# A causal mask as a bound on the score in the pass out of PSUM, and sixteen weight sums moved to layer 0's feed-forward

## The chip, the cores and the metric

The kernel runs on one core of one Trainium2 chip. The metric is the device time of one execution in microseconds (us), as the median of several runs; less is better.

The engines are named as in the profile: PE is TensorE (matrix multiply), PEld its weight loads, DVE is VectorE, ACT is ScalarE, POOL is GpSimd and SP is SyncE, which issues most transfers. POOL issues the rest. Each engine works through its own instructions in the order in which the program lists them.

## What is computed

One inference step of a two-layer decoder for a group of 1024 prompt tokens and 8 sample tokens, width 1024, all in float32. Layer 0 mixes by a gated linear recurrence beside attention into 256 memory tokens, layer 1 by stick-breaking attention over shared keys and values beside the same kind of memory attention. Each layer ends with a SwiGLU feed-forward of width 2816. The parts of the reference that the change touches:

```python
def swiglu(h, w_gu, w_down):
    gate, up = jnp.split(h @ w_gu, 2, axis=-1)
    return (jax.nn.silu(gate) * up) @ w_down
...
def stick_breaking(q, k, v, bias, q_pos, k_pos):
    ...
        z = jnp.einsum('bqhd,bkhd->bhqk', qi.astype(jnp.float32), kf) * scale + bf
        mask = (k_pos[None, :] < pi[:, None])[None, None]
        log_keep = jnp.where(mask, jax.nn.log_sigmoid(-z), 0.0)
        tail = lax.cumsum(log_keep, axis=3, reverse=True) - log_keep
        w = jnp.where(mask, jnp.exp(jax.nn.log_sigmoid(z) + tail), 0.0)
        return jnp.einsum('bhqk,bkhd->bqhd', w, vf)
```

## The kernel before

The prompt is worked in two groups of 512 tokens; group 1 also carries the 8 sample tokens, so its tiles are 520 wide. Every float32 matrix product is made of three products of rounded parts: a weight tile is loaded by SP (line 199), rounded by ACT (204), its remainder taken by DVE (205), and TensorE multiplies (218). Raw and split weights have five buffers each.

The program is written as generators, one for each piece of work. `weave` runs several of them together, each with a number that says into how many steps it is thought to fall; it always takes the one that is least far on. That sets the order of the instructions on each engine. A feed-forward is cut into parts (`PARTS`: 5, 5, 4, 4 and 4 tiles of 128 hidden columns).

Stick-breaking attention of a prompt group is `sb_prompt`. For each of four heads it goes through units of one or two query chunks of 128 tokens. The scores come into one of three PSUM banks (1314). DVE passes them out, adds the head's offset and bounds them at 44 (1319). ACT makes softplus of them, exp and then ln(1 + x) (1297, 1298). In the block of 128 x 128 on the diagonal DVE multiplies this by a 0/1 matrix `sm01` (1301), which takes away the tokens that may not be seen. A running sum from the right (1326), a subtraction (1328) and an exponential (1329) give the weights, and the diagonal block is multiplied by `sm01` once more. Then TensorE transposes (1338), ACT passes out of PSUM (1340) and TensorE multiplies by the values (1343). There are 32 diagonal blocks: four heads, two groups, four query chunks.

Memory attention of a prompt group (`mem_attn`) has scores at 854, their maximum at 859, a division at 871, transposes at 878. For the sample tokens, `sb_sample` and `mem_attn_sample` run on DVE: a key tile of 512 KB is loaded for each token (`c`; 941 for memory by SP, 953 by gathers on POOL for the paged keys and values, two halves each), the token's query is loaded spread over all partitions (`b<-qd`, 911), and DVE multiplies and reduces (912, 913). For the values it scales and adds (924, 925) and TensorE sums over the partitions (926). The tiles `c` have four buffers.

The second group's feed-forward is done with fewer products, from sums of blocks of the weights (`ffn_w`). Those sums are made by transfers from DRAM to DRAM that POOL issues: for each part eight steps, four of them copies or first terms (556) and four accumulating (554), in `weight_sums`. Ahead of each step stands a marker, a copy of one column of a tile that was just made (551, `mk`); POOL waits for that tile, and so the transfer starts no earlier. Layer 0 has sums for parts 2 to 4, layer 1 for all five parts. Layer 1's forty sums are used from the last stage on, in `ffn_w(1, ...)`.

The stages in which layer 1's sums stand before: sixteen (parts 0 and 1, 1.25 MB each) beside group 0's stick-breaking attention, eight (part 2, 1 MB) beside the weighted feed-forward of group 1 in layer 0, and sixteen (parts 3 and 4, 1 MB) beside group 1's stick-breaking attention and the samples' attention:

```python
    weave((chain(b0.sb(), b0.mem()), 25), (chain(f1.part(0), f1.part(1)), 18), (islice(ws, 16), 17))
...
    weave((chain(fw.part(2), fw.part(3), fw.part(4)), 24), (islice(ws, 8), 8))
```

The functions that the change touches:

Of the kernel before, what the change touches and what calls it, by code (L numbers as in the profile page):

```python
# [9 lines left out]
F32 = mybir.dt.float32  # L10
# [4 lines left out]
ALU = mybir.AluOpType  # L15
# [3 lines left out]
P = 128  # L19
# [4 lines left out]
def tile_decoder(  # L24
# [6 lines left out]
    nc = tc.nc  # L31
# [25 lines left out]
    const = pool("const", 1)  # L57
# [83 lines left out]
    ones = const.tile([P, P], F32, name="ones")  # L141
# [25 lines left out]
    def drain(*gens):  # L167
        for g_ in gens:
            for _ in g_:
                pass  # L170

    def chain(*gens):
        for g_ in gens:
            yield from g_

    def weave(*streams):

        live = [[0, n, g_] for g_, n in streams]
        while live:
            cur = min(live, key=lambda e: e[0] / e[1])  # L180
            cur[0] += 1
            try:
                next(cur[2])
            except StopIteration:
                live.remove(cur)
# [1111 lines left out]
        nc.scalar.activation(e[:, :w], zb[:, :w], AF.Exp)  # L1297
        nc.scalar.activation(e[:, :w], e[:, :w], AF.Ln, bias=1.0)

    def keep_strict(t):  # L1300
        nc.vector.tensor_mul(t, t, sm01)

    def sb_prompt(g, Qs, xo):

        units = [[(0, g), (2, g)], [(1, g)], [(3, g)]]
# [3 lines left out]
        def weights(h, kh, unit, first):  # L1309
            ps, spans, o = S(), [], 0  # L1310
            for c, s in unit:
                w = (c + 1) * P if s == g else G
                spans.append((c, s, o, w))
                nc.tensor.matmul(  # L1314
                    ps[:, o : o + w], Qs[h // 2][:, h % 2, c * P : (c + 1) * P], kh[:, s, :w], start=True, stop=True
                )
                o += w
            zb = B()
            nc.vector.tensor_scalar(zb[:, :o], ps[:, :o], biasp[:, h : h + 1], 44.0, op0=ALU.add, op1=ALU.min)
            e = B()  # L1320
            softplus(zb, e, o)
            for c, s, a, w in spans:
                if s == g:
                    keep_strict(e[:, a + w - P : a + w])
                d = e[:, a : a + w][:, ::-1]
                nc.vector.tensor_tensor_scan(d, d, d, first.get(c, 0.0), op0=ALU.add, op1=ALU.max)
                first[c] = e[:, a : a + 1]
            nc.vector.tensor_sub(zb[:, :o], zb[:, :o], e[:, :o])
            nc.scalar.activation(zb[:, :o], zb[:, :o], AF.Exp)
            for c, s, a, w in spans:  # L1330
                if s == g:
                    keep_strict(zb[:, a + w - P : a + w])
            return zb, spans, o

        def values(vh, po, zb, spans, n):
# [97 lines left out]
    with tc.issue_after(made[0].ins):  # L1433
        trif = const.tile([P, P], F32, name="trif")
        nc.gpsimd.affine_select(
            trif, ones, pattern=[[-1, P]], compare_op=ALU.is_ge, fill=0.0, base=0, channel_multiplier=1
        )

        sm01 = const.tile([P, P], F32, name="sm01")
        nc.gpsimd.affine_select(  # L1440
            sm01, ones, pattern=[[-1, P]], compare_op=ALU.is_gt, fill=0.0, base=0, channel_multiplier=1
        )
        sel = const.tile([P, NB, NB], F32, name="sel")
        nc.gpsimd.affine_select(
# [1 line left out]
            compare_op=ALU.is_equal, fill=0.0, base=0, channel_multiplier=0,  # L1446
# [61 lines left out]
    weave((a1.core(), 22), (f0.part(0), 9), (islice(w0, 8), 9))  # L1508
    a1.open()
    weave((a1.sample(), 6), (a1.gate(), 4), (f0.part(1), 9), (w0, 5))  # L1510
    weave((chain(a1.merge(), a1.mem()), 12), (a1.mem_sample(), 20), (chain(f0.part(2), f0.part(3)), 16))
    drain(f0.part(4))
    xk0, xb0 = [], []
    o1 = out_proj(1, 0, M)
    drain(o1.mm(a1.xo, 0, 1))
# [5 lines left out]
    weave((b0.heads(), 8), (o1.finish(), 17))  # L1521
    b0.open()
    f1 = ffn(1, 0, o1.x)
    ws = weight_sums(1, range(5))
    weave((chain(b0.sb(), b0.mem()), 25), (chain(f1.part(0), f1.part(1)), 18), (islice(ws, 16), 17))
    set_banks(True)
    fw = ffn_w(0, o1.x, (5, 6, 5), 2, False, f1.R)
# [13 lines left out]
    f0 = ffn(0, 1, o0.x)  # L1541
    weave(
        (chain(b1.sb(), b1.mem()), 45), (chain(b1.sb_sample(), b1.mem_sample()), 39),
        (chain(f0.part(0), f0.part(1), f0.part(2), f0.part(3)), 34), (ws, 17),
    )
    o1 = out_proj(1, 1, A, True)
    drain(o1.mm(b1.xo))
# [37 lines left out]
```

## Time and profile before

| | |
|---|---|
| median of three runs | 2513.66 us (2510.47 to 2513.87) |
| profiled execution | 2513.78 us; its span, first to last instruction, 2511.9 us |
| mean granted TensorE clock | 0.995 |
| busy | PE 98%, PEld 86%, DVE 64%, ACT 48%, POOL 5% of the span |
| DMA | 41.4% of sixteen engines' span for SP's queue, 13.4% for POOL's |

Where a line of the profile reads `x64 | 17.0, 287 | 15.1 <-ACT b L1298 11.5`, there were 64 such instructions, busy for 17.0 us together, 287 ns each in the mean; their engine had stood idle for 15.1 us just before them, and what ended 11.5 us of that was ACT's instruction of line 1298. In a line of waits, `PE s L1338 <- DVE b L1301: 5.0, 3, 4.5` says that PE's instruction of line 1338, which writes a tile `s`, waited 5.0 us in all for DVE's of line 1301, three times, at most 4.5 us. In a line by time, the first two numbers are the start and the duration in us, and the bracket is idle time and what ended it. The granted clock is the share of its full clock that TensorE was given.

### The profile page before, as it was taken

How to read it: one execution, taken by the hardware profiler on the slowest of the kernel's cores; microseconds unless marked ns; L12 is line 12 of the kernel's file. 1: busy time of each engine (PE TensorE's matmuls, PEld its weight loads, DVE VectorE, ACT ScalarE, POOL GpSimd, SP SyncE). 2: the span in 40 equal slices, each digit the busy share in tenths (PEclk: the TensorE clock that was granted, in tenths of full speed). 3: DMA queues.
4: the chain of work that ended last, by engine and by line, in shares of the span. 5: the costliest groups of instructions: out<-in, count | busy, mean ns of one | idle time of the engine just before them, and what ended most of it. 6: DMA issues, size and time to landing. Idle time of an engine off the chain costs nothing.

```text
span 2511.9 us, 40889 instructions
## 1 busy us (share of the span) xinstructions
PE 2467.7 (98%) x15455; PEld 2160.5 (86%) x15455; DVE 1609.2 (64%) x2900; ACT 1197.4 (48%) x2289; POOL 119.6 (5%) x187
## 2 busy tenths in 40 slices
PE   8999999999999999999999999999999999999998
PEld 6888888877877898999999989876677798999998
DVE  5766556654766576665655676776687538845666
ACT  5437543243433454554434554554454335554445
POOL 1000000000000000010100100021000000000000
PEclk9999999999999999999999999999999999999999
DMA  5355656554743447476767746575456643464552
GB/s 189 116 158 126 162 174 164 130 145 144 195 122 101 130 138 219 148 181 163 187 177 194 221 139 191 167 193 143 135 167 169 167 123 118 134 186 140 150 151 73
DMA packets 521550, 391.24 MB, mean 156 GB/s; under 512 B 19973, under 2 KB 459858, under 8 KB 521354
## 3 DMA queue, kind: packets, MB, share of 16 engines
q1 hardware_dynamic: 493194, 308.94, 41.4%
q0 software_dynamic: 28160, 79.70, 13.4%
q8 instruction: 121, 1.98, 0.3%
q14 instruction: 75, 0.61, 0.1%
HBM read 358.76 MB, written 101.11 MB: 183 GB/s over the span
## 4 chain that ended last, share of the span: by engine, by line
PE 90%; DVE 4%; DMA 3%; ACT 1%; issue 1%; SPq 0%; POOL 0%; DVEq 0%; ACTq 0%
PE mm L218 53%; PE q L499 11%; PE q L631 7%; PE q L453 2%; PE s L1150 2%; PE mm L1018 2%; DMA b<-qd 1%; PE s L1343 1%; PE s L885 1%; PE s L854 1%; PE mm L803 1%; PE mm L830 1%; PE s L1314 1%; PE q L663 1%; PE ns L926 1%
## 5 line engine op out<-in xcount | busy, mean ns | idle before, releaser
L218 PE MATMUL mm<-x,ws 128*128 128x512 f32 (+1 forms) x6624 | 1216.0, 340 | 2.4 <-DVE t L235 1.5
L218 PEld LDWEIGHTS mm<-x,ws 128*128 128x128 f32 x6624 | 1013.6, 189 | 155.5 <-issue 17.4
L204 ACT CAST ws<-w 128x512 fp32r<-128x512 f32 (+1 forms) x672 | 395.1, 589 | 616.8 <-PE mm L218 468.3
L205 DVE TENSOR_TENSOR ws<-w,ws 128x512 fp32r<-128x512 f32 (+1 forms) x672 | 435.1, 651 | 259.7 <-ACT ws L204 247.5
L218 PE MATMUL mm<-m,ws 128*128 128x512 f32 (+1 forms) x1536 | 329.3, 367 | 0.0
L218 PEld LDWEIGHTS mm<-m,ws 128*128 128x128 f32 x1536 | 255.1, 189 | 51.3 <-issue 1.9
L631 PE MATMUL q<-m,ws 128*128 128x260 f32 x1440 | 175.7, 283 | 0.0
L631 PEld LDWEIGHTS q<-m,ws 128*128 128x128 f32 x1440 | 173.4, 188 | 0.9 <-DVE t L522 0.5
L490 DVE TENSOR_TENSOR ws<-w,ws 128x512 fp32r<-128x512 f32 x164 | 112.4, 691 | 79.7 <-ACT ws L489 77.1
L489 ACT CAST ws<-w 128x512 fp32r<-128x512 f32 x164 | 101.4, 621 | 98.8 <-PE q L631 33.1
L499 PE MATMUL q<-x,ws 128*128 128x260 f32 x1008 | 134.3, 282 | 0.0
L499 PEld LDWEIGHTS q<-x,ws 128*128 128x128 f32 x1008 | 126.4, 188 | 0.0
L499 PE MATMUL q<-y,ws 128*128 128x260 f32 x912 | 119.3, 283 | 0.1
L499 PEld LDWEIGHTS q<-y,ws 128*128 128x128 f32 x912 | 113.5, 189 | 0.3 <-ACT q L506 0.3
L235 DVE TENSOR_SCALAR t<-mm 128x512 f32<-128x512 f32 (+1 forms) x70 | 48.4, 691 | 57.6 <-PE mm L218 57.3
L695 DVE TENSOR_TENSOR t<-t,mm 128x512 f32<-128x512 f32 (+1 forms) x54 | 37.2, 689 | 60.0 <-PE mm L218 59.9
L390 DVE TENSOR_TENSOR r<-r,mm 128x512 f32<-128x512 f32 (+1 forms) x72 | 49.4, 686 | 39.9 <-PE mm L218 39.0
L239 DVE TENSOR_TENSOR t<-t,t 128x512 f32<-128x512 f32 (+1 forms) x54 | 37.4, 693 | 55.4 <-ACT t L238 55.4
L226 DVE TENSOR_TENSOR m<-t,m 128x512 fp32r<-128x512 f32 (+1 forms) x88 | 61.0, 693 | 6.8 <-ACT m L225 5.3
L225 ACT CAST m<-t 128x512 fp32r<-128x512 f32 (+1 forms) x88 | 54.9, 624 | 21.7 <-DVE t L695 13.0
L453 PE MATMUL q<-x,ws 128*128 128x260 f32 x480 | 61.0, 288 | 3.7 <-DVE r L390 2.2
L258 DVE TENSOR_TENSOR st<-st,n 128x512 f32<-128x512 f32 (+1 forms) x91 | 62.4, 694 | 2.9 <-ACT n L257 1.5
(342 smaller groups left out, 2869.1 us busy)
## 6 DMA issues: line engine op xcount, KB each, us to landing
w<-in_w_gu SPq DMA_DIRECT2D x310, 256.0 KB, 3.2
w<-in_w_down SPq DMA_DIRECT2D x160, 256.0 KB, 2.9
wsum<-in_w_gu POOLq DMA_DIRECT2D x36, 1024.0 KB, 9.6
w<-wsum SPq DMA_DIRECT2D x94, 256.0 KB, 3.3
w<-in_w_in_a SPq DMA_DIRECT2D x80, 256.0 KB, 3.2
w<-in_w_o SPq DMA_DIRECT2D x64, 256.0 KB, 2.8
wsum<-in_w_gu POOLq DMA_DIRECT2D x12, 1280.0 KB, 10.5
wsum<-wsum POOLq DMA_DIRECT2D x12, 1024.0 KB, 6.6
```

Source lines behind the costliest of these rows:

```text
L204: nc.scalar.copy(ws[:, 0, :n, :], raw[:, :n, :])
L205: nc.vector.tensor_sub(ws[:, 1, :n, :], raw[:, :n, :], ws[:, 0, :n, :].bitcast(F32))
L218: nc.tensor.matmul(ps[:, a, : PW[g]], wt, xt[k][:, xi, o : o + PW[g]], start=(k == 0 and wi == 0), stop=(k == nk - 1 and wi == 2),)
L225: nc.scalar.copy(dst[0], src)
L226: nc.vector.tensor_sub(dst[1], src, dst[0].bitcast(F32))
L258: nc.vector.tensor_add(acc[:, :n], acc[:, :n], t[:, :n])
L453: ins = nc.tensor.matmul(pp[a][:, :h], wt, xt[k][:, xi, a * h : (a + 1) * h], start=(k == 0 and wi == 0), stop=(k == ND - 1 and wi == 2),)
L489: nc.scalar.copy(w[:, 0, :], src)
L490: nc.vector.tensor_sub(w[:, 1, :], src, w[:, 0, :].bitcast(F32))
L499: nc.tensor.matmul(ps[:, :h], w[:, wj, k * P : (k + 1) * P], x[:, xi, :], start=(first and k == 0 and wi == 0), stop=(k == 3 and wi == 2), ...
L631: nc.tensor.matmul(pp[a][:, :h], wt, mids[k][:, xi, a * h : (a + 1) * h], start=(k == 0 and wi == 0), stop=(k == nf - 1 and wi == 2),)
L1018: nc.tensor.matmul(pb[i][:, a, :], xt[k][:, xi, c * P : (c + 1) * P], ws[:, s, :], start=(k == 0 and wi == 0), stop=(k == ND - 1 and wi == 2),
```

## The change

The mask. A matrix `cap` of 128 x 128 holds 44 where a token may be seen and -300 where not; POOL fills it at the start. In the pass out of PSUM the diagonal block is taken by an instruction with three operands, which adds the offset and bounds the score by `cap` element by element. The columns beside it are passed as before, in an instruction of their own. Both multiplications by `sm01` go: at -300 softplus is 0 and so is the weight.

The sums. `ws` is begun earlier: eleven steps beside layer 0's memory attention of group 1 and of the samples and parts 2 and 3 of group 0's feed-forward, five beside its part 4. The next sixteen (now parts 2 and 3) and eight (part 4) stand in the stages that had sixteen and eight before, and none is left for group 1's stick-breaking attention.

```diff
-    def keep_strict(t):
-        nc.vector.tensor_mul(t, t, sm01)
-
...
             zb = B()
-            nc.vector.tensor_scalar(zb[:, :o], ps[:, :o], biasp[:, h : h + 1], 44.0, op0=ALU.add, op1=ALU.min)
+            bh, i = biasp[:, h : h + 1], 0
+            for c, s, a, w in spans:
+                if s != g:
+                    continue
+                j = a + w - P
+                if i < j:
+                    nc.vector.tensor_scalar(zb[:, i:j], ps[:, i:j], bh, 44.0, op0=ALU.add, op1=ALU.min)
+                i = j + P
+                nc.vector.scalar_tensor_tensor(zb[:, j:i], ps[:, j:i], bh, cap, op0=ALU.add, op1=ALU.min)
+            if i < o:
+                nc.vector.tensor_scalar(zb[:, i:o], ps[:, i:o], bh, 44.0, op0=ALU.add, op1=ALU.min)
             e = B()
             softplus(zb, e, o)
             for c, s, a, w in spans:
-                if s == g:
-                    keep_strict(e[:, a + w - P : a + w])
                 d = e[:, a : a + w][:, ::-1]
...
             nc.scalar.activation(zb[:, :o], zb[:, :o], AF.Exp)
-            for c, s, a, w in spans:
-                if s == g:
-                    keep_strict(zb[:, a + w - P : a + w])
             return zb, spans, o
...
-        sm01 = const.tile([P, P], F32, name="sm01")
+        cap = const.tile([P, P], F32, name="cap")
+        nc.gpsimd.memset(cap, 44.0)
         nc.gpsimd.affine_select(
-            sm01, ones, pattern=[[-1, P]], compare_op=ALU.is_gt, fill=0.0, base=0, channel_multiplier=1
+            cap, cap, pattern=[[-1, P]], compare_op=ALU.is_gt, fill=-300.0, base=0, channel_multiplier=1
         )
...
-    weave((chain(a1.merge(), a1.mem()), 12), (a1.mem_sample(), 20), (chain(f0.part(2), f0.part(3)), 16))
-    drain(f0.part(4))
+    ws = weight_sums(1, range(5))
+    weave(
+        (chain(a1.merge(), a1.mem()), 12), (a1.mem_sample(), 20), (chain(f0.part(2), f0.part(3)), 16),
+        (islice(ws, 11), 11),
+    )
+    weave((f0.part(4), 8), (islice(ws, 5), 5))
...
-    ws = weight_sums(1, range(5))
...
-        (chain(f0.part(0), f0.part(1), f0.part(2), f0.part(3)), 34), (ws, 17),
+        (chain(f0.part(0), f0.part(1), f0.part(2), f0.part(3)), 34),
```

How this moves instructions is shown at three places. In the names, `mk` is a marker, `wsum` a sum, `c` a sample token's tile, `m` and `r` tiles of the feed-forward; the numbers after them count tiles and shift between the two programs.

POOL's order in group 1's stick-breaking attention, where the samples' value pages are gathered, before:

```order
L953 DMA c_16960<-in_cache_sb_v,pidx 128x512 x2
L551 COPY mk_16556<-m_16553 128x1
L554 DMA wsum_16091<-in_w_gu 512x512
L953 DMA c_17070<-in_cache_sb_v,pidx 128x512 x2
L551 COPY mk_16738<-r_16587 128x1
L554 DMA wsum_16089<-in_w_gu 512x512
...
L953 DMA c_17568<-in_cache_sb_v,pidx 128x512
L551 COPY mk_17178<-m_17175 128x1
L554 DMA wsum_16090<-in_w_gu 512x512
L953 DMA c_17568<-in_cache_sb_v,pidx 128x512
L953 DMA c_17654<-in_cache_sb_v,pidx 128x512 x2
```

and now:

```order
L953 DMA c_16977<-in_cache_sb_v,pidx 128x512 x2
L953 DMA c_17086<-in_cache_sb_v,pidx 128x512 x2
L953 DMA c_17194<-in_cache_sb_v,pidx 128x512 x2
L953 DMA c_17335<-in_cache_sb_v,pidx 128x512 x2
L953 DMA c_17443<-in_cache_sb_v,pidx 128x512 x2
L953 DMA c_17552<-in_cache_sb_v,pidx 128x512 x2
L953 DMA c_17575<-in_cache_sb_v,pidx 128x512 x2
L953 DMA c_17657<-in_cache_sb_v,pidx 128x512 x2
```

The markers and the sums are gone from between the gathers.

POOL's order from layer 0's last own sum on, before; the next marker belongs to group 0's stick-breaking attention:

```order
L551 COPY mk_5812<-r_4587 128x1
L554 DMA wsum_4532<-in_w_gu 512x512
L551 COPY mk_9423<-m_9416 128x1
L556 DMA wsum_9421<-in_w_gu 512x640
L551 COPY mk_9578<-m_9575 128x1
```

and now, where the tiles `m` and `r` of the markers are those of group 0's feed-forward in layer 0, parts 2 to 4:

```order
L551 COPY mk_5815<-r_4590 128x1
L554 DMA wsum_4535<-in_w_gu 512x512
L551 COPY mk_6166<-m_6159 128x1
L556 DMA wsum_6164<-in_w_gu 512x640
L551 COPY mk_6259<-m_6253 128x1
L556 DMA wsum_6162<-in_w_gu 512x640
L551 COPY mk_6358<-m_6346 128x1
L554 DMA wsum_6164<-in_w_gu 512x640
L551 COPY mk_6495<-r_4590 128x1
L554 DMA wsum_6162<-in_w_gu 512x640
```

Sixteen sums of 640 columns have come in ahead of those that stood next.

DVE's order around the first unit of the first head in group 0, with two diagonal blocks, before (`s` is the score bank, 235 a step of the feed-forward beside it):

```order
L1319 TENSOR_SCALAR b_9277<-s_9274,biasp 128x512
L205 TENSOR_TENSOR ws_9451<-w_9449,ws_9451 128x512
L1301 TENSOR_TENSOR b_9279<-b_9279,sm_177 128x128 x2
L1326 SCALAR_TENSOR_TENSOR b_9279<-b_9279 128x128
L1326 SCALAR_TENSOR_TENSOR b_9279<-b_9279 128x384
L1328 TENSOR_TENSOR b_9277<-b_9277,b_9279 128x512
L205 TENSOR_TENSOR ws_9456<-w_9454,ws_9456 128x512
L1301 TENSOR_TENSOR b_9277<-b_9277,sm_177 128x128 x2
L235 TENSOR_SCALAR t_9349<-mm_9300 128x520
```

and now (1322, 1324, 1331 and 1333 are the plain pass, the bounded pass, the running sum and the subtraction in the changed code):

```order
L1324 SCALAR_TENSOR_TENSOR b_9336<-s_9333,biasp,cap 128x128
L1322 TENSOR_SCALAR b_9336<-s_9333,biasp 128x256
L1324 SCALAR_TENSOR_TENSOR b_9336<-s_9333,biasp,cap 128x128
L205 TENSOR_TENSOR ws_9507<-w_9505,ws_9507 128x512
L1331 SCALAR_TENSOR_TENSOR b_9340<-b_9340 128x128
L1331 SCALAR_TENSOR_TENSOR b_9340<-b_9340 128x384
L1333 TENSOR_TENSOR b_9336<-b_9336,b_9340 128x512
L205 TENSOR_TENSOR ws_9512<-w_9510,ws_9512 128x512
L235 TENSOR_SCALAR t_9406<-mm_9357 128x520
```

One pass out of PSUM has become three, and the four multiplications ahead of the running sum and behind the exponential are gone.

## The prediction

> **What bounds the kernel now.** I read the page first: busy shares and the chain that ended last, for the engine that sets the time; then the waits of that engine; then the stretches in which they lie.
>
> ```profile
> span 2511.9 us, 40889 instructions
> PE 2467.7 (98%) x15455; PEld 2160.5 (86%) x15455; DVE 1609.2 (64%) x2900; ACT 1197.4 (48%) x2289; POOL 119.6 (5%) x187
> PE 90%; DVE 4%; DMA 3%; ACT 1%; issue 1%; SPq 0%; POOL 0%; DVEq 0%; ACTq 0%
> ```
>
> TensorE is busy 98% of the span and carries 90% of the chain. An edit that leaves its matmuls alone, as this one does, can return only TensorE's waits and the time at a lowered clock. DVE at 64% has room: its busy time as such is worth nothing, only what stands in its queue ahead of something that TensorE needs. So the question is where TensorE waits. Three stretches bear on the change: 626 to 890 us (layer 0's feed-forward parts 2 to 4 of the first token group, where sixteen sums now go), 1027 to 1253 (stick-breaking attention of group 0), 1590 to 2010 (that of group 1 with the sample tokens, which the sums leave).
>
> ```profile
> 626.00:890.00 264.00, 264.00 (x1197) 208.38 (x1197) 169.00 (x268) 111.00 (x207) 1.02 (x1) 1.00 0.46 135
> 1027.00:1253.00 226.00, 223.22 (x1733) 212.47 (x1731) 139.79 (x281) 114.93 (x233) 22.26 (x32) 1.00 0.68 172
> 1590.00:2010.00 420.00, 402.24 (x1820) 304.55 (x1819) 291.00 (x456) 193.34 (x369) 45.09 (x56) 0.98 0.59 163
> ```
>
> (Columns: stretch, its length; busy time of PE, PEld, DVE, ACT, POOL; granted clock; DMA share; GB/s.) TensorE is never idle in the first, 2.8 us in the second, 17.8 us in the third, where alone the granted clock is below 1.00. The first has the lowest DMA share, 0.46. TensorE's waits in the third, then its only row in the second:
>
> ```profile
> PE s L1343 <- ACT b L1340: 5.1, 2, 3.9
> PE s L1338 <- DVE b L1301: 5.0, 3, 4.5
> PE s L878 <- DVE b L871: 4.4, 2, 2.5
> PE s L1314 <- DVE b L1319: 2.5, 1, 2.5
> PE s L1338 <- ACT b L1329: 0.6, 2, 0.4
> ```
> ```profile
> PE s L1338 <- DVE b L1301: 1.2, 3, 0.7
> ```
>
> The 4.5 us is put down to the mask multiply L1301, which this change removes. In order of time it has another root:
>
> ```profile
> 1744.15 0.97 POOL L953 DMA_INDIRECT c<-in_cache_sb_v,pidx  x1 [17.20 <-PE ns L926]
> 1745.46 1.14 POOL L554 DMA_DIRECT2D wsum<-in_w_gu  x1
> 1746.90 1.05 POOL L953 DMA_INDIRECT c<-in_cache_sb_v,pidx  x1 [0.31 <-issue]
> 1756.42 1.23 DVE L924 TENSOR_TENSOR c<-c,sc 128x1024 f32<-128x1024 f32 x1 [8.11 <-DMA c<-in_cache_sb_v,pidx]
> 1762.26 0.49 DVE L1301 TENSOR_TENSOR b<-b,sm 128x128 f32<-128x128 f32 x2
> 1762.69 1.09 PE L1338 MATMUL s<-ident,b 128*128 128x128 f32 x4 [4.47 <-DVE b L1301]
> ```
>
> A sum (L554) was issued between the two halves of a page gather; the second half took from 1746.90 to about 1756.4, DVE stood 8.11 us for it in its strict order, the masks queued behind, and TensorE behind them. The other long waits have the same shape:
>
> ```profile
> 1693.49 1.23 DVE L912 TENSOR_TENSOR c<-c,b 128x1024 f32<-128x1024 f32 x1 [2.34 <-DMA b<-qd]
> 1697.74 2.08 PE L1343 MATMUL s<-b,a 128*128 128x128 f32 x8 [3.90 <-ACT b L1340]
> 1719.73 1.22 DVE L924 TENSOR_TENSOR c<-c,sc 128x1024 f32<-128x1024 f32 x1 [3.86 <-DMA c<-in_cache_sb_v,pidx]
> 1726.79 1.13 PE L1314 MATMUL s<-a,a 128*128 128x512 f32 x2 [2.46 <-DVE b L1319]
> 1916.93 1.23 DVE L912 TENSOR_TENSOR c<-c,b 128x1024 f32<-128x1024 f32 x1 [3.15 <-DMA b<-qd]
> 1921.06 0.30 PE L878 MATMUL s<-ident,b 128*128 128x128 f32 x1 [2.46 <-DVE b L871]
> ```
>
> So I put to the sums 5.1 (L1343), the 4.5, 2.5 (L1314) and 4.4 (L878): 16.5 us. DVE's waits for transfers there, which lead to them, and below them its largest in the first stretch:
>
> ```profile
> DVE c L912 <- DMA b<-qd: 13.8, 9, 3.2
> ...
> DVE c L924 <- DMA c<-in_cache_sb_v,pidx: 12.0, 2, 8.1
> ...
> DVE c L924 <- DMA c<-in_cache_mem_v: 8.1, 5, 3.6
> ```
> ```profile
> DVE c L924 <- DMA c<-in_cache_mem_v: 5.8, 4, 2.7
> ```
>
> That is 33.9 us of DVE waiting for 16.5 us of TensorE: 0.49 for each. Waits cost twice, since the clock falls after them (pieces just behind four of them):
>
> ```profile
> 1697.00:1704.50 7.50, 6.76 (x24) 6.01 (x25) 5.31 (x11) 2.45 (x8) 1.33 (x2) 0.54 0.47 143
> 1727.00:1732.00 5.00, 5.00 (x18) 3.90 (x18) 4.31 (x6) 3.29 (x6) 0.00 (x0) 0.66 0.91 302
> 1761.00:1766.00 5.00, 3.31 (x8) 1.26 (x9) 3.98 (x9) 3.78 (x7) 0.14 (x1) 0.66 0.37 105
> 1919.00:1932.00 13.00, 8.98 (x43) 7.10 (x43) 9.57 (x17) 5.39 (x14) 1.18 (x2) 1.00 0.60 192
> ```
>
> The share missing is 0.46 x 7.5 + 0.34 x 5 + 0.34 x 5 = 6.9 us; the two waits around 1921 cost no clock. With the waits: 23.4 us hang on the sums.
>
> **The parts of the change and their sum.** First, the sums leave group 1's attention. What a load takes with and without them shows in the landing times (least, median, most) of L941's loads, in the third stretch and then in the first, where one sum alone was issued:
>
> ```profile
> DMA to landing us min/median/max: 3.8/3.9/9.2
> ```
> ```profile
> DMA to landing us min/median/max: 4.3/4.5/4.6
> ```
>
> With 4.5 us in place of 9.5 the half gather of 1746.90 ends the 8.11 us wait 5 us earlier, more than the 4.47 that TensorE stood. The bounds of the gain are 0 (other work is as late) and 23.4. I take four fifths, 18.7: where a wait of DVE is longer than what the sum added, a part stays, and with TensorE earlier another step of the same chains comes due; the evictions L1319 behind the sample work are late next.
>
> Second, the sums arrive in the first stretch: sixteen transfers of 1.25 MB on POOL's queue, with their markers (a copy of one column). Nothing of POOL's waits behind them there; no gather stands in that part of its order. Beside them lie SP's weight loads and the loads for the samples' memory attention. What an accumulating and a copying sum of that size take to land:
>
> ```profile
> wsum<-in_w_gu POOLq DMA_DIRECT2D x12, 1280.0 KB, 10.5
> ...
> wsum<-wsum POOLq DMA_DIRECT2D x4, 1280.0 KB, 6.1
> ```
>
> Eleven of them over some 200 us, at 6.1 to 10.5 us, are in flight nearly half the time, so about four of the eight value loads (L941) land later, by up to 9.2 - 4.5 = 4.7 us: at an estimate of 3.5 each, some 14 us more of DVE waiting. At 0.49 that is 7 us of TensorE; by the 8.1 us of the same kind in the third stretch, to which none of the long TensorE waits above belongs, 0. I take 3.5, and one fall of the clock, 1.7 (0.34 x 5): 5 us. Bounds: 0 and the 23.4 that the sums cost now; less than 0 is excluded, TensorE waits for nothing there. The five sums beside part 4 meet no sample work: weight loads run ahead into five buffers, and cost 0; without that cover they would be in the same bound. The sums that stay in group 0's attention shrink from 1.25 to 1 MB: 0.
>
> TensorE's rule bears on the clock's share. The Trainium skill (TensorE: Matmul & The Clock Gate, Part 1) says that the clock halves after about 3.4 us of idle window and advises against gaps over some 3 us. Here a wait of 2.46 us was followed by 0.66 and another of 2.46 by 1.00, so the trace agrees with its free-running window, not with a gap that short being safe. By the advice alone the new place would pay no 1.7 and the forecast would be lower by as much; by the rows I keep it.
>
> Third, the mask. Its rows, with the nearest to the new operation (three operands, one of them in PSUM, 128 x 128):
>
> ```profile
> L1319 DVE TENSOR_SCALAR b<-s,biasp 128x512 f32<-128x512 f32 x32 | 23.9, 746 | 7.9 <-PE s L1314 7.8
> ...
> L1301 DVE TENSOR_TENSOR b<-b,sm 128x128 f32<-128x128 f32 x64 | 17.0, 287 | 15.1 <-ACT b L1298 11.5 <-ACT b L1329 2.9
> ...
> L1190 DVE SCALAR_TENSOR_TENSOR b<-b,a,s 128x128 f32<-128x128 f32 x16 | 5.6, 347 | 0.5
> L1319 DVE TENSOR_SCALAR b<-s,biasp 128x256 f32<-128x256 f32 x8 | 3.9, 481 | 1.4 <-PE s L1314 1.2
> ```
>
> 64 multiplies of 287 ns go: 18.4 us. 32 three-operand evictions of 347 come: 11.1. The plain evictions lose 128 columns at each diagonal block, (746 - 481)/256 = 1.04 ns a column: 4.2 less. DVE does 11.5 us less, beside other work. On the path a unit with two diagonal blocks evicts 347 + 481 + 347 - 746 = 0.43 us longer and loses 4 x 287 = 1.15 on the way to its transposes; a unit with one loses 0.57 and pays about 0.21. TensorE's transposes L1338 then wait for ACT's exponential directly. Of L1338's waits 1.2 us in group 0 and about 1 in group 1 are left after the 4.5; I take 1.5 off. The other bound is a loss: if TensorE waited for every longer eviction, 8 heads x (0.43 + 0.21 + 0.21) = 6.8 us; L1314's single wait of 2.5 came from a gather, so I stay near the gain. One more fill on POOL at the start: 0, behind the first row loads.
>
> Sum: -18.7 + 5 - 1.5 = -15.2 us. The profiled execution took 2513.8 us (1.9 around its span), 0.1 from the median of the three, 2513.7. So 2498.6 us. A measurement of this kernel can tell about 0.2%, 5 us.
>
> **Rivals.** A: the stalls move along. The same sums delay the value loads where they go, and TensorE loses there what it gained: only the mask is left, 2512.3. The Trainium skill (DMA: Bandwidth & Descriptors, Issuing engines are not separate DMA queues) has all queues interleave on the same 16 engines, which would speak for this and give A's time. For it stand the four waits of L924 that exist there already; against it, that no gathers share POOL's queue there and that the 5.8 us of them cost TensorE nothing.
>
> B: everything comes back and the new place is free: 2513.8 - 23.4 - 1.5 = 2488.9. For it, DMA share 0.46 and no TensorE wait there; against it, chains in order rarely give back all.
>
> C: the mask costs. The longer evictions hold the three score banks of PSUM: 2513.8 - 18.7 + 5 + 6.8 = 2506.9.
>
> D, slower: all eight value loads fall behind sums and land at 9.2 instead of 4.5 us: 37.6 us of DVE standing, with the feed-forward's PSUM evictions queued behind L924. At 0.49 that is 18.4 us, with clock falls in the ratio 6.9 to 16.5 another 7.7: 26.1 - 18.7 - 1.5 = +5.9, 2519.7. It decides once the new place costs over 20.2 us, more than 1.26 for each sum, against 1.46 (23.4/16) in the old. For it, that 1.46; against it, the shorter chain between load and TensorE there.
>
> **How the numbers follow.** The forecast, 2491 to 2506: 0.62. B 0.12, C 0.05, A 0.15, D 0.06. Faster: 0.62 + 0.12 + 0.05 = 0.79; same 0.15; slower 0.06. From B's 2488.9 to C's 2506.9 lies 0.79; up to 2511 a third of A is added, so the range is 2488 to 2511.
>
> **What would show it.** Right: L924's wait for sb_v pages falls from 12.0 to under 3 us, TensorE's waits in group 1's attention from 17.6 to under 5, granted clock there 1.00; in the first stretch DVE's wait for mem_v rises to 15 to 20 us and TensorE's from 0 to 2 to 5; DVE's busy time falls by some 11 us. Wrong: waits of L1314 for its eviction in many units (C); TensorE's rows for L390 or L235 in the first stretch above 15 us (A, D); waits in group 1's attention that stay without any sum in flight, which would put the fault with the gathers and not with the sums.

## The result, and the profile after

The changed kernel takes 2495.35 us (median of four runs, 2491.38 to 2497.11) against 2513.57 for the kernel before on the same chip: a ratio of 0.9929, 95% interval 0.9913 to 0.9944. The forecast was 2498.6, 3.2 us too slow; the sign, the place of the gain and the price of the old place hold, three smaller terms do not. Of all executions behind the numbers below one, of the kernel with 16 full extra transfers, took 4883.74 us; its ratio is taken without it.

The page of the changed kernel, its span and busy times (the profile is of the slowest of the four executions, 2497.11 us):

```profile
span 2495.4 us, 40868 instructions
PE 2461.4 (99%) x15455; PEld 2155.8 (86%) x15455; DVE 1598.1 (64%) x2868; ACT 1196.8 (48%) x2289; POOL 121.9 (5%) x188
```

DVE's busy time fell by 11.1 us, nearly what the mask's operations add up to (11.5), and TensorE's by 6.3, about the 6.9 us that the prediction read as time at a lowered clock. The same three stretches of the work as in the prediction, shifted to where they now lie (columns as there):

```profile
626.00:900.00 274.00, 266.65 (x1206) 209.15 (x1205) 168.92 (x270) 111.27 (x209) 24.45 (x34) 1.00 0.77 206
1036.00:1258.00 222.00, 221.34 (x1723) 211.30 (x1722) 134.52 (x264) 114.78 (x233) 19.82 (x32) 1.00 0.62 156
1594.00:1990.00 396.00, 393.91 (x1814) 299.52 (x1813) 284.75 (x439) 192.67 (x369) 26.56 (x24) 1.00 0.44 131
```

The third is the gain: idle time of TensorE 2.1 us in place of 17.8, clock 1.00 in place of 0.98, DMA share 0.44 in place of 0.59. The first is the price: idle 7.35 us in place of 0, share 0.77 in place of 0.46. TensorE's largest wait in the first stretch, and that of the third:

```profile
PE mm L218 <- DVE r L390: 6.2, 3, 3.0
```
```profile
PE s L1340 <- ACT b L1334: 1.6, 5, 0.5
```

And DVE's waits for transfers, in the first and then in the third:

```profile
DVE c L924 <- DMA c<-in_cache_mem_v: 14.7, 6, 4.5
...
DVE c L912 <- DMA b<-qd: 8.0, 2, 7.6
```
```profile
DVE c L924 <- DMA c<-in_cache_sb_v,pidx: 5.8, 4, 2.1
```

The page gathers still come late four times, by 2.1 us at most, but TensorE's longest wait in that stretch is 0.5 us. The 7.6 us in the new place was not foreseen. In order of time (the wait of 3.03 is TensorE's longest there):

```profile
704.50 1.04 POOL L554 DMA_DIRECT2D wsum<-in_w_gu  x1
709.89 0.66 POOL L556 DMA_DIRECT2D wsum<-wsum  x1
710.35 0.99 SPq L911 DMA_DIRECT2D b<-qd  x2
721.23 1.22 DVE L912 TENSOR_TENSOR c<-c,b 128x1024 f32<-128x1024 f32 x1 [7.61 <-DMA b<-qd]
723.11 3.04 PE L218 MATMUL mm<-m,ws 128*128 128x512 f32 x12 [3.03 <-DVE r L390]
```

Two queries of sample tokens are asked for just behind two sums and land some 10 us later; DVE stands for the first in its strict order, the feed-forward's eviction L390 is queued behind it, and TensorE waits for that.

Both programs have 15455 matmuls, in the same order but for 130 places, none of which is used here; so the start of the same matmul in each says where the difference arises. It grows by 8.7 us from matmul 3860 (679.2 before, 679.7 after) to 5018 (917.1, 926.4), falls by 1.4 to 6948 (1209.3, 1217.2), by 3.9 at the start of the weighted feed-forward (7334: 1260.4, 1264.5), and by 22.6 from 10036 (1627.6, 1631.9) to 11580 (1987.3, 1969.0); 1.5 are given back by the start of the last stage (12738: 2179.3, 2162.5), where the granted clock was 0.84 over 11 us (2128 to 2139) and at the same place before 1.00 (2146 to 2157), with the same waits of 1.4 and 0.9 us around it.

### The profile page after: what moved, and what is told of

Its sections match the earlier page's. It is cut to its first block, busy times and chain, and to the rows that moved or that the text cites. A ratio compares the mean times of both kernels' runs of the same rounds, so it can differ in the third digit from the quotient of the medians.

```text
span 2495.4 us, 40868 instructions
## 1 busy us (share of the span) xinstructions
PE 2461.4 (99%) x15455; PEld 2155.8 (86%) x15455; DVE 1598.1 (64%) x2868; ACT 1196.8 (48%) x2289; POOL 121.9 (5%) x188
## 3 DMA queue, kind: packets, MB, share of 16 engines
q0 software_dynamic: 28160, 79.70, 13.5%
## 4 chain that ended last, share of the span: by engine, by line
PE 92%; DVE 4%; DMA 2%; ACT 1%; issue 1%; SPq 0%; DVEq 0%; ACTq 0%
PE mm L218 54%; PE q L499 11%; PE q L631 7%; PE s L1150 2%; PE mm L1018 2%; PE q L453 2%; PE s L1345 1%; PE s L1311 1%; PE s L885 1%; PE s L854 1%; PE mm L803 1%; PE mm L830 1%; PE q L663 1%; DMA c<-in_cache_mem_v 1%; PE ns L926 1%
## 5 line engine op out<-in xcount | busy, mean ns | idle before, releaser
L205 DVE TENSOR_TENSOR ws<-w,ws 128x512 fp32r<-128x512 f32 (+1 forms) x672 | 434.5, 650 | 270.5 <-ACT ws L204 263.8
L390 DVE TENSOR_TENSOR r<-r,mm 128x512 f32<-128x512 f32 (+1 forms) x72 | 49.3, 685 | 37.1 <-PE mm L218 36.2
L258 DVE TENSOR_TENSOR st<-st,n 128x512 f32<-128x512 f32 (+1 forms) x91 | 62.2, 691 | 3.0 <-ACT n L257 1.6
```

What stands on the lines that cost most here:

```text
L205: nc.vector.tensor_sub(ws[:, 1, :n, :], raw[:, :n, :], ws[:, 0, :n, :].bitcast(F32))
L258: nc.vector.tensor_add(acc[:, :n], acc[:, :n], t[:, :n])
```

## The experiments

The theory: a sum's traffic makes the samples' just-in-time loads land late, DVE stands for them in its order, TensorE waits behind DVE and the clock falls. The rivals: the order on POOL and the waits for markers cost, not the traffic; the mask holds part of the gain; the new place costs for another reason than the sample loads. Each ratio is to the kernel before, on the same chip.

| run | us | ratio | 95% interval |
|---|---|---|---|
| changed kernel | 2495.35 | 0.9929 | 0.9913 to 0.9944 |
| mask alone | 2508.23 | 0.9983 | 0.9974 to 0.9992 |
| sums alone | 2501.95 | 0.9956 | 0.9944 to 0.9968 |
| 16 small extra transfers in group 1's attention | 2495.98 | 0.9932 | 0.9919 to 0.9945 |
| 16 full extra transfers there | 2516.37 | 1.0011 | 1.0002 to 1.0019 |
| all 16 sums beside part 4 | 2510.47 | 0.9989 | 0.9980 to 0.9998 |
| the same, markers off the tiles r | 2512.34 | 0.9997 | 0.9988 to 1.0006 |
| 6 sums early, 10 beside part 4 | 2495.14 | 0.9930 | 0.9917 to 0.9943 |
| 10 beside part 4, 14 beside the weighted feed-forward | 2493.79 | 0.9932 | 0.9918 to 0.9946 |
| 5 beside part 4, 19 beside the weighted feed-forward | 2486.08 | 0.9891 | 0.9877 to 0.9906 |
| second mask multiplication put back | 2496.42 | 0.9935 | 0.9921 to 0.9948 |
| first put back | 2495.45 | 0.9932 | 0.9918 to 0.9945 |
| both put back | 2499.68 | 0.9947 | 0.9933 to 0.9961 |

### The parts apart

The mask alone: the changed kernel with the sums as they stood.

```diff
-    ws = weight_sums(1, range(5))
     weave(
         (chain(a1.merge(), a1.mem()), 12), (a1.mem_sample(), 20), (chain(f0.part(2), f0.part(3)), 16),
-        (islice(ws, 11), 11),
     )
-    weave((f0.part(4), 8), (islice(ws, 5), 5))
+    drain(f0.part(4))
...
+    ws = weight_sums(1, range(5))
...
-        (chain(f0.part(0), f0.part(1), f0.part(2), f0.part(3)), 34),
+        (chain(f0.part(0), f0.part(1), f0.part(2), f0.part(3)), 34), (ws, 17),
```

> Only the mask of the change: the bound in the pass out of PSUM, with all forty sums where they stood before. Theory (the sums carry the gain, the mask takes only a few small waits of L1338): 2510.5 to 2512.5 us, 1 to 3 us under the kernel before; the 8 us wait of DVE for a page half behind a sum and TensorE's wait of some 4 us after it stay, only under another name, since L1301 is gone. Rival (the mask multiplies themselves held TensorE, as the row PE s L1338 <- DVE b L1301 reads): 5 us or more under before, 2505 to 2508, and TensorE's waits in group 1's attention fall from 17.6 to about 12 us.

Measured: 0.9983, about 4.3 us, between the two. TensorE's waits in group 1's attention, in the profile of the fastest execution (2503.49 us):

```profile
PE s L1345 <- ACT b L1342: 6.1, 3, 4.1
PE s L1340 <- ACT b L1334: 4.0, 6, 2.4
PE s L878 <- DVE b L871: 3.5, 2, 1.9
PE s L1311 <- DVE b L1324: 1.4, 1, 1.4
```

They add up to 15.0 us in place of 17.6: the long ones are all still there, the longest at 4.1 in place of 3.9, and the one put down to L1301 has gone on under ACT's name (L1334 is the exponential), at 2.4 in place of 4.5. Most of the stalls were not the mask's; still it is worth more than the 1.5 us of the forecast.

The sums alone: the old pass out of PSUM and both multiplications again, with the sums where the change puts them.

```diff
-                nc.vector.scalar_tensor_tensor(zb[:, j:i], ps[:, j:i], bh, cap, op0=ALU.add, op1=ALU.min)
...
+            nc.vector.tensor_scalar(zb[:, :o], ps[:, :o], biasp[:, h : h + 1], 44.0, op0=ALU.add, op1=ALU.min)
...
+                if s == g:
+                    keep_strict(e[:, a + w - P : a + w])
```

> Only the move of the sixteen sums: the old mask with its 64 multiplications stays. Theory: 2497 to 2499.5 us, 2 to 4 above the changed kernel (2495.4); group 1's attention has TensorE waits of 2 to 5 us instead of 17.6 and a granted clock of 1.00. Rival (half the gain is the mask's): 2503 to 2507, with L1338 still waiting 4 to 5 us for L1301.

Measured: 0.9956, about 11.1 us, over the theory's band and under the rival's. The two parts make 15.4 of the 17.8 that both give (0.0071 of 2513); the rest is within the intervals. By the starts of the matmuls they nearly add up in group 1's attention (10036 to 11580): 17.5 us for the sums alone, 4.6 for the mask alone, 22.6 for both. What the old mask still costs with the sums gone shows at one place. DVE there, then TensorE:

```profile
1728.69 1.22 DVE L924 TENSOR_TENSOR c<-c,sc 128x1024 f32<-128x1024 f32 x1 [2.58 <-DMA c<-in_cache_sb_v,pidx]
1729.83 0.28 DVE L1301 TENSOR_TENSOR b<-b,sm 128x128 f32<-128x128 f32 x1
```
```profile
1730.17 0.48 PE L1338 MATMUL s<-ident,b 128*128 128x128 f32 x1 [2.83 <-DVE b L1301]
```

A page that is late without any sum, and behind it in DVE's order the unit's last mask multiplication, for which TensorE waits 2.83 us. Just after it the clock was 0.87 over 13 us, 1.7 us more:

```profile
1727.00:1740.00 13.00, 10.18 (x43) 8.27 (x42) 5.97 (x9) 4.57 (x8) 0.00 (x0) 0.87 0.22 72
```

### Traffic or order in the old place

Sixteen extra transfers put back into group 1's attention of the changed kernel, with markers, first of 32 rows each, then of 512. Nothing uses what they make.

```diff
-        (chain(f0.part(0), f0.part(1), f0.part(2), f0.part(3)), 34),
+        (chain(f0.part(0), f0.part(1), f0.part(2), f0.part(3)), 34), (idle_sums(range(3, 5), 32), 17),
```

> The changed kernel with sixteen extra transfers in group 1's attention, at the places in POOL's order where before had its sums, with the same markers, but of 32 rows (64 KB) in place of 512; their results are not used. Theory (the traffic of the sums is what cost there): 2495 to 2498 us, as the changed kernel. Rival (the order on POOL and the waits for the markers between the page gathers cost, whatever the transfers carry): 2505 or more, with DVE waiting 8 us or more for sb_v pages.

> The same sixteen extra transfers in group 1's attention in full size (512 rows, 1 MB), results not used: more traffic than either kernel has. Theory: what before paid there comes back, some 17 us: 2511 to 2518, DVE waiting 8 us or more for sb_v pages, TensorE some 12 to 18 us in that stage at a lowered clock. Rival (the order alone): the same time as with the small transfers. Rival (neither; the gain came from elsewhere): 2495 to 2500.

Measured: 2495.98 and 2516.37 us. The small ones cost nothing that can be told; the full ones cost 0.0082 of 2513, 20.6 us, 1.3 a transfer. So it is the traffic, not the order or the markers. The full ones bring back the whole picture: the stage's window, then DVE's wait for pages and TensorE's longest waits in it (lines are 20 higher here: L944 is L924, L1365 is L1345):

```profile
1590.00:2015.00 425.00, 408.04 (x1843) 308.59 (x1843) 287.36 (x445) 193.51 (x372) 45.05 (x56) 0.98 0.58 163
```
```profile
DVE c L944 <- DMA c<-in_cache_sb_v,pidx: 11.7, 3, 7.9
```
```profile
PE s L1365 <- ACT b L1362: 7.1, 4, 4.9
```

### The new place

No sum beside the samples' memory attention, all sixteen beside part 4, where no sample work stands:

```diff
-    weave(
-        (chain(a1.merge(), a1.mem()), 12), (a1.mem_sample(), 20), (chain(f0.part(2), f0.part(3)), 16),
-        (islice(ws, 11), 11),
-    )
-    weave((f0.part(4), 8), (islice(ws, 5), 5))
+    weave((chain(a1.merge(), a1.mem()), 12), (a1.mem_sample(), 20), (chain(f0.part(2), f0.part(3)), 16))
+    weave((f0.part(4), 8), (islice(ws, 16), 16))
```

> The changed kernel, but none of the sixteen sums beside layer 0's memory attention of the samples: all of them beside part 4 of group 0's feed-forward, where no sample work stands. Theory (the 8.6 us that the stretch 626 to 890 now takes longer come from the samples' key, value and query loads falling behind sums): the 8.6 us come back, 2486 to 2489, and no TensorE wait for L390 is left there. Rival (sums cost wherever they stand, by the transfers' share of the DMA engines or because part 4's own weight loads are late): 2493 to 2500, with TensorE waiting for weight splits (L204, L205) in part 4.

Measured: 2510.47 us, 15 slower than the changed kernel and beyond both bands, on the rival's side. The 8.7 us did come back where the sums had left: TensorE is busy the whole of the first row here. But part 4 and what follows it take 27 us longer (from matmul 4632 to 5018), the second row:

```profile
668.00:857.00 189.00, 189.00 (x816) 145.30 (x815) 117.50 (x187) 76.91 (x149) 6.72 (x11) 1.00 0.52 147
857.00:945.00 88.00, 69.12 (x409) 61.59 (x408) 45.92 (x71) 33.03 (x57) 12.24 (x20) 0.88 1.02 273
```

DMA share 1.02 as the profile counts it, and 19 us of TensorE's waiting. Two causes offered themselves, in TensorE's and in DVE's waits:

```profile
PE mm L218 <- DVE ws L205: 12.4, 3, 9.1
```
```profile
DVE r L371 <- POOL mk L551: 21.0, 3, 9.1
```

Weight splits that come late, and 21.0 us in which DVE's in-place step on a tile r waited until POOL's marker had copied a column of it, while POOL itself stood behind an unfinished sum. The second looked the larger, so it was taken away: the markers of that place copy a column of a constant in place of one of r.

```diff
-                now[0] = self.R[m][:, 0:1]
+                now[0] = ident[:, 0:1] if free[0] else self.R[m][:, 0:1]
...
+    free[0] = True
     weave((f0.part(4), 8), (islice(ws, 16), 16))
+    free[0] = False
```

> All sixteen sums beside part 4, as in the run that took 2510.5 us, but there the markers behind the down projection copy a column of a constant in place of one of the tiles r. Theory (a marker that stands on POOL behind an unfinished sum holds the tile r that it reads, DVE's in-place step L371 on r waits for it, 21.0 us in that run, and TensorE behind it): the 21.0 us wait goes and most of the 27 us come back, 2490 to 2498; what is left is weight loads that land late. Rival (the DMA engines are full there, share 1.02, and late weight loads alone hold TensorE): 2505 to 2511, with TensorE still waiting 10 us or more for weight splits L205.

Measured: 2512.34 us; the theory of the markers fell. DVE's wait for them is gone and nothing came back. The rival is nearest, 1.3 us short of the time and with 9.1 of its 10 us for L205. The same window, then the largest wait of ACT and the two largest of TensorE:

```profile
857.00:945.00 88.00, 68.43 (x414) 61.27 (x413) 46.40 (x72) 33.46 (x58) 11.98 (x21) 0.88 1.07 279
```
```profile
ACT ws L204 <- DMA w<-in_w_o: 34.9, 10, 5.7
```
```profile
PE mm L218 <- DVE ws L205: 9.1, 2, 6.4
PE ns L247 <- DVE st L258: 6.9, 1, 6.9
```

The DMA engines are full for 88 us, and the weights of the output projection come when they can. The Trainium skill (DMA: Bandwidth & Descriptors, Issuing engines are not separate DMA queues) says that transfers of all issuing engines interleave on the same sixteen engines; here sums on POOL's queue hold up weights on SP's, and the trace agrees.

Fewer of them, and earlier:

```diff
-        (islice(ws, 11), 11),
+        (islice(ws, 6), 22),
...
-    weave((f0.part(4), 8), (islice(ws, 5), 5))
+    weave((f0.part(4), 8), (islice(ws, 10), 10))
```

> The changed kernel, but six of the sixteen sums in the first quarter of the stretch with the samples' memory attention and ten beside part 4. Theory (only sums that are in flight together with the samples' just-in-time loads cost): the late waits around 721 and 803 us go, 2487 to 2490, within 2 us of the kernel with all sixteen beside part 4. Rival (any sum beside sample work costs in proportion, 8.6 us for eleven): six keep 4.7 us, 2490.5 to 2492.5.

Measured: 2495.14 us, no change, beyond both bands. Six sums hit the same query load as eleven did (DVE's waits, 668 to 868 us):

```profile
DVE c L912 <- DMA b<-qd: 7.1, 1, 7.1
DVE c L924 <- DMA c<-in_cache_mem_v: 6.0, 3, 3.0
```

The starts of the matmuls divide the price. In the changed kernel 5.4 us arise around the query load (matmul 4000 to 4100, 712.2 to 740.1 us) and 3.2 behind it, where value loads are late. With the six, the value loads fell to 6.0 us of DVE's waiting, as without any sum (5.8 before), and nothing arises behind the query load; but 6.2 us arise around it, and 3.7 before it (3940 to 3980), where a weight tile is late:

```profile
689.99 0.62 ACT L204 CAST ws<-w 128x512 fp32r<-128x512 f32 x1 [6.83 <-DMA w<-in_w_down]
```

Here the first three sums were issued at 663.70, 664.64 and 674.65, in the changed kernel at 666.86, 678.27 and 688.23, without that wait. The price is thus not so much a sum: a single load that misses its time, the query, makes 5.4 to 6.9 us of it in all eight profiles with sums beside it.

### Away from the samples altogether

Two kernels leave the samples' memory attention without sums and put them beside part 4 and the weighted feed-forward instead: ten and fourteen, five and nineteen. The second as a diff; the first has 10 and 14 in place of 5 and 19:

```diff
     weave(
         (chain(a1.merge(), a1.mem()), 12), (a1.mem_sample(), 20), (chain(f0.part(2), f0.part(3)), 16),
-        (islice(ws, 11), 11),
     )
     weave((f0.part(4), 8), (islice(ws, 5), 5))
...
-    weave((chain(fw.part(2), fw.part(3), fw.part(4)), 24), (islice(ws, 8), 8))
+    weave((chain(fw.part(2), fw.part(3), fw.part(4)), 24), (islice(ws, 19), 19))
```

> The changed kernel with no sum beside layer 0's memory attention of the samples: ten of the forty beside part 4 of group 0's feed-forward, sixteen beside group 0's stick-breaking attention as now, fourteen (now eight) beside the weighted feed-forward. Theory (the 8.6 us of the new place are the samples' loads behind sums; ten beside part 4 keep POOL's markers ahead of the in-place steps on the tiles r): 2486 to 2489. Rivals: the ten crowd part 4 as sixteen did, with DVE's L371 waiting for markers: 2492 to 2500; or the six added beside the weighted feed-forward make its weight loads late: 2491 to 2496, TensorE waiting there for L205.

> As the one before, but five beside part 4 (as in the changed kernel) and nineteen beside the weighted feed-forward. Theory: 2485.5 to 2488.5, at or a little under ten and fourteen. Rival (the weighted feed-forward, which loads weights and its own sums, pays for eleven more): 2491 to 2498.

Measured: 2493.79 and 2486.08. The second, inside its theory's band, is the fastest kernel of this study, 27 us under before and about 9 under the change. The first lies in its rivals' bands, but neither rival's wait is in its trace: DVE's L371 waits for no marker, and TensorE for no L205 beside the weighted feed-forward. With ten, one load spoils it. POOL and SP by time, then ACT, for which TensorE waited 6.5 us behind the normalization (L258):

```profile
889.09 1.03 POOL L554 DMA_DIRECT2D wsum<-in_w_gu  x1 [7.17 <-DVE r L371]
889.94 1.29 POOL L556 DMA_DIRECT2D wsum<-in_w_gu  x1
892.47 0.64 POOL L556 DMA_DIRECT2D wsum<-in_w_gu  x1
896.23 0.38 SPq L199 DMA_DIRECT2D w<-in_w_o  x1
```
```profile
911.68 0.62 ACT L204 CAST ws<-w 128x512 fp32r<-128x512 f32 x1 [8.58 <-DMA w<-in_w_o]
```

Three sums within 3.4 us: an accumulating one and the two first terms of the next part, which depend on nothing before them. A weight tile asked for behind them, at 896.23, was what ACT waited for until 911.68; the one weight load there for which a landing is shown, issued at 901.17, took 13.5 us. In the run with six and ten, whose ten cost 0.6 us in the same place, the sums there were issued 5 to 12 us apart (868.28, 873.33, 881.44, 892.41, 904.34, 914.67). That the burst makes the difference is read from these two traces and from the late tile w_down above; it was not tried by itself.

With five, the new places by window:

```profile
626.00:857.00 231.00, 231.00 (x1023) 180.71 (x1022) 149.24 (x239) 96.15 (x183) 3.38 (x5) 1.00 0.50 145
857.00:930.00 73.00, 72.91 (x472) 65.42 (x472) 55.24 (x86) 38.60 (x66) 4.07 (x6) 1.00 0.71 195
1255.00:1530.00 275.00, 273.14 (x2082) 261.39 (x2082) 167.09 (x299) 126.44 (x237) 32.13 (x46) 1.00 0.82 219
```

Nothing in the first two; in the third, with a DMA share of 0.82, nineteen sums in place of eight cost about 2 us at most (from matmul 7334 to 10036 the lead on before shrinks from 5.5 to 3.35; kernels with eight lose 0.0 to 1.4 there). That stage has weight loads that run ahead, and none for sample tokens.

### Which part of the mask

The multiplications put back into the changed kernel, the second (shown), the first likewise ahead of the running sum, and both:

```diff
             nc.scalar.activation(zb[:, :o], zb[:, :o], AF.Exp)
+            for c, s, a, w in spans:
+                if s == g:
+                    nc.vector.tensor_mul(zb[:, a + w - P : a + w], zb[:, a + w - P : a + w], sm01)
```

> The changed kernel with the second multiplication by the 0/1 matrix put back behind the exponential (it changes no result there). Theory (the mask's gain is mostly this one: a DVE operation between ACT's exponential and TensorE's transposes has to queue behind DVE's sample work): 2499 to 2502 us, 4 to 6.5 above the changed kernel, about all that the old mask costs (2502.0 against 2495.4), with TensorE's transposes L1338 waiting 3 us or more for it in group 1's attention. Rival (DVE's busy time is what counts, half of it in each multiplication): 2497 to 2499.

> The changed kernel with the first multiplication by the 0/1 matrix put back ahead of the running sum (it changes no result there). Theory (this one only lengthens a chain that has slack behind it): 2495 to 2497.5 us. Rival (each multiplication has half of the mask's gain): 2497.5 to 2500.

> The changed kernel with both multiplications by the 0/1 matrix put back, so that of the mask's change only the pass out of PSUM in pieces stays. Put back one by one they gave 2496.4 and 2495.5 us against 2495.4, while the whole old mask gives 2502.0. Theory (the two together are what the old mask costs: either alone finds slack behind the late value pages, both do not): 2500 to 2503 us, with TensorE's transposes waiting about 3 us for DVE at the place of the one late page around 1728 us. Rival (neither multiplication matters; the old pass of the whole 512 columns, or the order that the shorter passes give the work, makes the difference): 2494 to 2498.

Measured: 2496.42, 2495.45 and 2499.68. By time either alone is inside the spread, and the second stays under its theory's band. Both together cost 0.0018 of 2513, 4.5 us, of the 6.8 by which the sums alone stay behind the changed kernel, but its interval overlaps the changed kernel's. The starts of the matmuls tell more. Around the late page, from matmul 10440 to 10516 (1718.3 and 1735.1 us in the changed kernel), the six other profiles with the new mask and no full sums there take as long as the changed kernel to 0.1 us. With the first multiplication put back it is 1.4 us longer, with the second 3.3, with both 3.0, and with the whole old mask 4.5. So the second has most of it, as its theory said, and the slack that the other two theories give to either alone is not there. TensorE's transposes with the second alone, then with the first alone:

```profile
1726.18 0.47 PE L1343 MATMUL s<-ident,b 128*128 128x128 f32 x1 [1.67 <-DVE b L1337]
```
```profile
1727.42 0.66 PE L1342 MATMUL s<-ident,b 128*128 128x128 f32 x4 [1.74 <-ACT b L1336]
```

With the second (L1337), the granted clock was 0.86 over the 12 us from 1726, 1.7 us more, and with the old mask 0.87; with the first (L1336 is the exponential) it was 1.00. With both it was 1.00 too, and the trace has this at the place of the late page (1331, 1339 are the multiplications, 1333 the running sum, 1335 the subtraction, 1336 the exponential, 1345 the transposes), DVE and then TensorE:

```profile
1724.81 1.22 DVE L1333 TENSOR_TENSOR_SCAN b<-b 128x512 f32<-128x512 f32 x1
1728.50 1.23 DVE L924 TENSOR_TENSOR c<-c,sc 128x1024 f32<-128x1024 f32 x1 [2.47 <-DMA c<-in_cache_sb_v,pidx]
1729.65 0.68 DVE L1335 TENSOR_TENSOR b<-b,b 128x512 f32<-128x512 f32 x1
```
```profile
1731.05 0.55 PE L1345 MATMUL s<-ident,b 128*128 128x128 f32 x3 [2.89 <-ACT b L1336]
```

In the changed kernel the running sum is followed at once by the subtraction, at 1725.30, ahead of the late page:

```profile
1725.30 0.69 DVE L1333 TENSOR_TENSOR b<-b,b 128x512 f32<-128x512 f32 x1
1727.86 1.23 DVE L924 TENSOR_TENSOR c<-c,sc 128x1024 f32<-128x1024 f32 x1 [1.86 <-DMA c<-in_cache_sb_v,pidx]
```

With both back, and with the first alone, the subtraction has slipped behind L924 in DVE's order; with the second alone, that multiplication stands behind it. `weave` alone does not set this order, since its steps are the same in these programs. So one operation of 0.28 us more in a unit's chain cost 1.4 or 3.3 us, where it brought the step for which TensorE waits to the other side of an instruction that waits for a transfer.

## Why the prediction came out as it did

**The bound.** Right: TensorE's work did not change; what came back was waiting and lowered clock.

**The sums leave group 1's attention: -18.7.** Right, and nearly in size. In the trace of the sums alone the stretch gains 17.5 us, three quarters of the 23.4 and not four fifths. The times say 15.9: 11.1 for the sums alone, with the 8.7 that they pay in the new place added and the 3.9 of the weighted feed-forward (below) taken off. The full extra transfers cost 20.6 us by the runs, in a kernel with the new mask. In the changed kernel the stretch gained 22.6, since most of the mask's gain lies in it. Of the signs, the waits for pages fell to 5.8 us and not under 3: late pages did not vanish, they became short enough to be nearly hidden.

**The sums arrive: +5.** The mechanism was right, the size 8.7. The sum had eight value loads, four of them 3.5 us late; the trace has 14.7 us of DVE waiting for them, a little under the 15 to 20 forecast, and 7.3 us of TensorE's waiting, over the 2 to 5. Left out was the other load of the same loop, the query b<-qd, that had cost DVE 13.8 us in the old place, in a row that the prediction quotes: 7.61 us at once, TensorE's 3.03 behind it, and 5.4 of the 8.7 by the starts of the matmuls. The 1.7 us for one fall of the clock did not come in this profile, where the clock stayed at 1.00; in five of the six others with the same eleven sums it was 0.98 or 0.99 over 668 to 868 us. "The five sums beside part 4 cost 0" holds (the difference there does not move), and so does the condition set to it, that without the loads' lead they would cost like the others: ten cost 7.9, sixteen 27 us.

**The sums that stay beside group 0's attention: 0.** Wrong: 3.9 us were gained behind them. Before, the weighted feed-forward's first weights were late beside the last sums of 1.25 MB, ACT waited for them, and TensorE paid (the kernel before around 1255 us, waits of ACT, then of TensorE, then the window):

```profile
ACT ws L489 <- DMA b<-in_w_gu: 7.2, 1, 7.2
```
```profile
PE q L453 <- DVE r L390: 2.2, 1, 2.2
```
```profile
1250.00:1260.00 10.00, 7.79 (x54) 7.61 (x53) 5.65 (x10) 5.97 (x11) 0.00 (x0) 0.83 1.01 277
```

2.2 of waiting and 0.17 x 10 = 1.7 of clock. After, the sums there are of 1 MB and neither is left; every kernel with the moved sums gains 3.6 to 3.9 there. The mask alone, with 1.25 MB, kept a wait of 2.1 and lost only the clock's part. Whether it is the sums' size or their moment was not tried apart.

**The mask: -1.5.** Too small: 4.3 by its own run, 6.8 on top of the moved sums, 6.5 by the starts of the matmuls. In group 0's attention it gained 1.4, about the 1.2 of L1338's waits there; in group 1's 5.1 (22.6 - 17.5), nearly all around the one late page. The prediction bounded it by L1338's waits that were left after the 4.5 had been given to the sums. It took the chain's shortening as a length, and missed that it also changes which step stands behind a late page in DVE's order. The bound on the other side, the longer evictions, did not show: TensorE has no wait of L1311 for them in either stretch after.

**The sum.** By the starts of the matmuls the terms are -17.5 + 8.7 - 3.9 - 6.5 = -19.2 us in place of -15.2; in the profile the clock took 1.5 back at the end, and the ratio says 17.8 in all. That the forecast came within 3.2 us is in part luck: the arrival, 3.7 too small, and the weighted feed-forward, 3.9 left out, cancel.

**The rivals.** A (the stalls move along, 2512.3) and D (slower) did not come, though the kernel with all sixteen sums beside part 4 came out where A has its time, by weights in place of sample loads. B (all back, the new place free) has a time that the last placement passes, 2486.1 against 2488.9, though not by B's sum: the 3.9 and the mask's 6.5 are in it. C did not come.

## What to carry to other kernels

Background transfers should be placed by the lead of the loads beside them, not by the DMA share alone: nineteen sums in place of eight, at a share of 0.82, cost about 2 us at most beside weights that are loaded ahead, eleven at 0.77 cost 8.7 beside loads that an engine waits for in strict order, and sixteen cost 27 beside weights where the share reached 1.0. When transfers are moved, list every load of the loop that they come to stand beside, since a single one that misses its time can make more than half of the price. A wait's releaser in the profile is the last in a chain: the 21.0 us named for the marker brought nothing when they were taken away, and of the 4.5 named for the mask 2.4 stayed under another name. Where medians differ by less than their spread, the start of the same instruction in two traces can still tell a change of 1 or 2 us at its place.

## What the runs showed of the hardware

The clock's falls are partly chance. TensorE's only wait between 560 and 579 us, the same line in the changed kernel and in the one with ten and fourteen, and then the same place of the work behind it, 579 to 590 us, in the one and the other:

```profile
PE mm L218 <- DVE t L235: 1.5, 1, 1.5
```
```profile
579.00:590.00 11.00, 11.00 (x46) 7.39 (x45) 3.71 (x7) 2.87 (x6) 0.00 (x0) 0.84 0.69 196
```
```profile
579.00:590.00 11.00, 11.00 (x51) 7.67 (x52) 5.28 (x8) 4.33 (x7) 0.00 (x0) 1.00 0.62 188
```

The same wait, and a clock of 0.84 in one and 1.00 in the other: 0.16 x 11 = 1.8 us. Of fourteen profiles eight have a wait of 1.5 to 1.8 us there, and three of these the fall: the kernel before, the changed one, and the one with five and nineteen. Each of the three has a second fall around 610 us. So two profiles can differ by some 3 us where the programs do the same work (from matmul 3000 to 3860 the eleven others are 2.7 to 4.1 us faster). The Trainium skill (TensorE: Matmul & The Clock Gate, Part 1) calls the window of the gate free-running and says that the moment of its switching varies with where in the window the work begins. That the same wait is followed by a slow stretch in some profiles and not in others agrees with it. A fall belongs in a forecast as a chance, and the kernel with the fewest waits has the fewest chances.
